# Slots of an expert in another order: neighbouring places nine slots apart, from the other end in the second expert of a pair

## The chip, the cores and the metric

One Trainium2 chip, one of its cores. The metric is device time in microseconds (us) of one execution; the median of three runs of the kernel before is 708.25 us (707.63 to 709.4).

## The reference

One decoder block on 512 tokens of width 1024: an mLSTM branch and a differential-attention branch run beside each other and are merged, then comes a mixture of experts routed in two levels. The change touches only the last part, whose core is:

```python
g_idx = top_k(softmax(hf @ w_rg + b_rg), 1)          # one of 4 groups
j_idx = top_k(softmax(e_logits of that group), 2)    # two of its 8 experts
combine = sum(one_hot(e_idx, 32) * weights)
for e in range(32):
    act = silu(hf @ w_gate[e]) * (hf @ w_up[e])      # 1024 -> 256, twice
    y = y + combine[:, e:e + 1] * (act @ w_down[e])  # 256 -> 1024
```

Every token goes to two of the 32 experts, so there are 1024 pairs of token and expert. All weights are float32: 3 MB an expert, 100 MB in all.

## The kernel before

The kernel runs as one program on one core. First come the projections, the two branches and the output projection, as float32 products split into a high and a low part; they end near 440 us. Then routing is worked out (to about 462 us), and then the experts run in 16 pairs. Pair i holds the experts `eA[i]` and `eB[i] = eA[i] + 8`, which lie in different groups, so that no token is in both.

For each expert there are 64 slots (`CAP`, `LIM`). A slot stands for a row of the pair's 128-row output tile `y`: the first expert has partitions 0 to 63, the second 64 to 127. `pos` holds, for each token and expert, the token's place among the tokens of that expert, 1, 2, 3 and so on (0 where it does not go there). `sio` holds for each slot the place that it takes: before, 1 to 64 in order. `places_of(i)` compares `pos` with `sio` on VectorE and makes the one-hot matrix `oh` with which TensorE gathers the columns of the tokens (`gather_mm`). An expert with n tokens thus fills its first n slots; the others hold zeros.

`one_hots` makes, once, the one-hot matrices `orb` from the places `rk` of each token's two choices, and `slots` multiplies them with a small table `ev6` to get, for each slot of each pair, the token's row number (`ids`) and its weight (`wsl`). An empty slot gets the row number 1024.

For a pair (`experts`): 32 matmuls for gate and up into `gu`, SiLU on ScalarE, the product on VectorE, two transposes, then 8 matmuls with the down weights into two banks `o`, which VectorE scales into `y`. Between SiLU and the down product TensorE does the gather for pair i + 2. Then GpSimd issues an indirect DMA that adds the 128 rows of `y`, 4 KB each, to the rows `ids[:, i]` of the output in DRAM; a row number beyond 511 is skipped (`bounds_check`, `oob_is_err=False`). There are 16 such scatters.

The weights are loaded by SyncE (SP), 1 MB a load, six for a pair, in the order of use. Twenty tiles take them in turn; a load is issued when the tile's last reader is done, some 20 loads ahead of use at the beginning and 8 at the end (`ahead`). SP issues in order: a load that waits holds all behind it.

Around the change: `W2` hands out the seven small buffers of the pool `work` in turn. That pool is released before the experts, and the pool `moe` (two of the weight tiles, `y1`, the gathered columns) lies over it. `dc` is a pool for the dense stages; it is released before the output projection, and the tiles `y0` (x rows of the first 128 tokens, later one of the three `y`) and `wx0` lie over it. `brt` holds the 36 router biases and is read by one matmul in `mod2`.

Of the kernel before, what the change touches and what calls it, by code (L numbers as in the profile page):

```python
# [10 lines left out]
F32 = mybir.dt.float32  # L11
F32R = mybir.dt.float32r
BF = mybir.dt.bfloat16
# [3 lines left out]
ALU = mybir.AluOpType  # L17
# [11 lines left out]
LIM = 64  # L29
# [28 lines left out]
def block_kernel(ctx, tc, x, c, positions, w_ada, b_ada, norm1_w, w_in, b_igate, b_fgate, conv_w, conv_b,  # L58
# [3 lines left out]
    PE, V, S, G, SP = nc.tensor, nc.vector, nc.scalar, nc.gpsimd, nc.sync  # L62
# [5 lines left out]
    const = ctx.enter_context(tc.tile_pool(name="const", bufs=1))  # L68
# [3 lines left out]
    dc = tc.alloc_tile_pool(name="dense", bufs=1, side="right")  # L72
# [5 lines left out]
    def W2(name, shape, dt=F32):  # L78
        return wk.tile(shape, dt, name=name, tag="w2", bufs=7)
# [4 lines left out]
    def acc(name="acc"):  # L84
        return ps.tile([128, 512], F32, name=name, tag="acc", bufs=4)
# [82 lines left out]
    for i, w in enumerate((lam_q1, lam_k1, lam_q2, lam_k2)):  # L168
# [10 lines left out]
                    pattern=[[-1, 128]], channel_multiplier=1)  # L179
# [7 lines left out]
                    pattern=[[1, 128]], channel_multiplier=-1)  # L187
# [4 lines left out]
                    pattern=[[-1, 128]], channel_multiplier=1)  # L192
# [44 lines left out]

    io8 = const.tile([128, 8], F32, name="io8")
    G.iota(io8, pattern=[[1, 8]], base=-8, channel_multiplier=0, allow_small_or_imprecise_dtypes=True)
    sio = const.tile([128, 64], BF, name="sio")  # L240
    G.iota(sio, pattern=[[1, 64]], base=1, channel_multiplier=0, allow_small_or_imprecise_dtypes=True)
    if LIM < 64:
        G.memset(sio[:, LIM:], -1e6)
    pio = const.tile([128, 1], F32, name="pio")
    G.iota(pio, pattern=[[0, 1]], base=0, channel_multiplier=1, allow_small_or_imprecise_dtypes=True)
    tio = const.tile([128, 4], F32, name="tio")
# [4 lines left out]
                    pattern=[[1, 128]], channel_multiplier=-1)  # L251
# [27 lines left out]
    st = {}  # L279
# [562 lines left out]
    wr = const.tile([128, 8, 36], F32, name="wr")  # L842
    SP.dma_start(wr[:, :, 0:4], w_rg[0].rearrange("(j p) f -> p j f", p=128))
    SP.dma_start(wr[:, :, 4:36], w_re[0].rearrange("(j p) f -> p j f", p=128))
    brt = const.tile([1, 36], F32, name="brt")
    SP.dma_start(brt[:, 0:4], b_rg)
    SP.dma_start(brt[:, 4:36], b_re)
    gbc = []
# [495 lines left out]
    def dense():  # L1344
# [5 lines left out]
    bc = lambda ap, n: ap[:, :, None].to_broadcast([128, 4, n])  # L1350
# [3 lines left out]
    oh = {0: W2("oh", [128, 4, 128], F16),  # L1354
          1: st["y0"][:, 512:768].bitcast(F16).rearrange("p (t f) -> p t f", t=4)}
# [3 lines left out]
    def places_of(i, ts=slice(0, 4)):  # L1359
        n = ts.stop - ts.start  # L1360
        for h, e in enumerate((eA[i], eB[i])):
            V.tensor_tensor(oh[i if st.get("first") else 2][:, ts, h * 64:h * 64 + 64], sio[:, None, :].to_broadcast([128, n, 64]),  # L1362
                            pos[:, ts, e:e + 1].to_broadcast([128, n, 64]), op=ALU.is_equal)

    def columns_of(i):
# [51 lines left out]
    def first_places():  # L1417
        ranks(0)
        places_of(0, lo2)
        places_of(1, lo2)  # L1420
# [12 lines left out]
    ranks(2)  # L1433
    idle(W1[2], wm)
    places_of(0, hi2)
    weights()
    places_of(1, hi2)
# [10 lines left out]
    ys = [st["y0"], mo.tile([128, 1024], F32, name="y1"), gbc[0][:, 0]]  # L1448
# [14 lines left out]
    nmore = rt("nmore", [128, 1], I32)  # L1463


    orb = [ys[0][:, c * 128:c * 128 + 128].bitcast(BF).rearrange("p (t f) -> p t f", t=4) for c in range(2)]
    ev6 = [ys[1][:, c * 384:c * 384 + 384].bitcast(BF).rearrange("p (t n f) -> p t n f", t=4, n=6) for c in range(2)]
    wrf = wr.rearrange("p k f -> p (k f)")
    rk = wrf[:, 128:136].rearrange("p (a t) -> p a t", a=2)
# [28 lines left out]

    def one_hots():
        for c_ in range(2):  # L1500
            V.tensor_tensor(orb[c_], sio[:, None, :].to_broadcast([128, 4, 64]), bc(rk[:, c_], 64), op=ALU.is_equal)

    def slots():

        idp = st["idp"] = acc("idp")[:, 0:96].rearrange("p (n i) -> p n i", n=6)
        k = 0
        for t in range(4):
            for c_ in range(2):
                for h in range(2):
                    r_ = ev6[c_][:, t].rearrange("p n (a h j) -> p n a h j", a=2, h=2)[:, :, :, h]  # L1510
                    PE.matmul(idp[h * 64:(h + 1) * 64], orb[c_][:, t], r_, start=(k == 0), stop=(k == 7),
                              skip_group_check=True)
                k += 1

# [8 lines left out]
    def experts(first=False):  # L1523
# [15 lines left out]
        if first:  # L1539
            one_hots()  # L1540
            rounds()
        for i in range(16):
# [23 lines left out]
            if first and i == 0:  # L1566
                slots()
                slot_ids()
# [19 lines left out]
    with tc.For_i(0, more, 1):  # L1588
        V.tensor_scalar(rk, rk, -float(LIM), None, op0=ALU.add)
        V.tensor_scalar(pos, pos, -float(LIM), None, op0=ALU.add)  # L1590
        table()
        one_hots()
        slots()
        slot_ids()
        experts()
# [22 lines left out]
```

## Time and profile before

| what | value |
|---|---|
| median of three runs | 708.25 us |
| the profiled execution: time, and span of its instructions | 710.0 us, 708.2 us |
| mean granted TensorE clock | 0.988 of full speed |
| TensorE matmul busy | 676.4 us, 96% of the span |
| VectorE, ScalarE, GpSimd busy | 378.3, 234.4, 201.9 us |
| moved by DMA | 171.50 MB, mean 242 GB/s |
| of this by GpSimd's queue (scatters and a few small ones) | 5.28 MB, 3.7% of 16 engines over the span |

"PE" is TensorE's matmul, "PEld" its weight load, DVE VectorE, ACT ScalarE, POOL GpSimd, SPq the queue of SyncE. The DMA share is the mean busy share of the core's 16 DMA engines; packets that overlap can bring it above 1. Matmuls are pipelined, so their durations overlap. In a row of the timeline, the brackets hold the idle time of the engine before the instruction and what ended it.

### The profile page before, as it was taken

What the parts mean: (1) busy time and instruction counts of PE and PEld (TensorE: products, weight loads), DVE (VectorE), ACT (ScalarE), POOL (GpSimd) and SP (SyncE); (2) the same over time, 40 slices, a digit from 0 to 9 for tenths busy, and PEclk for the clock granted to TensorE, in tenths of its full rate; (3) what the DMA queues carried; (4) which work ended last, traced back from release to release, by engine and by line L of the source; (5) the groups of instructions that cost most, each with busy time, mean ns of one, the idle gap of its engine ahead of it and who ended that gap; (6) DMA issues with size and microseconds to landing.
All of it is one profiled execution on the core that took longest, in us unless ns stands there. A gap on an engine that the chain in (4) does not pass through costs nothing. (4 is left out here: it accounts for less than half of the span.)

```text
span 708.2 us, 11482 instructions
## 1 busy us (share of the span) xinstructions
PE 676.4 (96%) x4478; PEld 497.6 (70%) x4478; DVE 378.3 (53%) x767; ACT 234.4 (33%) x513; POOL 201.9 (29%) x208
## 2 busy tenths in 40 slices
PE   7999999999998999999999999899999999999972
PEld 4678877878777777778877888676667666766640
DVE  3557669766684467763696855853222332233211
ACT  5446772352442445543322234341111111111100
POOL 4213263436561213233244521431111121111100
PEclk9999999999999999999999999899999999999998
DMA  9974079225025011056646992898999999999981
GB/s 313 363 231 176 0 279 405 75 70 184 35 71 179 1 60 61 1 187 219 232 150 220 421 398 90 323 410 326 379 364 385 410 403 375 392 371 399 408 299 22
DMA packets 47402, 171.50 MB, mean 242 GB/s; under 512 B 8025, under 2 KB 16354, under 8 KB 33006
## 3 DMA queue, kind: packets, MB, share of 16 engines
q1 hardware_dynamic: 44526, 165.41, 60.4%
q0 software_dynamic: 2752, 5.28, 3.7%
q8 instruction: 37, 0.61, 0.3%
q14 instruction: 23, 0.19, 0.1%
q10 hardware_dynamic: 64, 0.02, 0.0%
HBM read 164.37 MB, written 10.51 MB: 247 GB/s over the span
## 5 line engine op out<-in xcount | busy, mean ns | idle before, releaser
L435 POOL TENSOR_TENSOR hl<-wp,hl 128x512 fp32r<-128x512 f32 x60 | 84.8, 1414 | 174.1 <-ACT hl L434 165.5
L434 ACT ACTIVATE hl<-wp 128x512 fp32r<-128x512 f32 x120 | 74.5, 628 | 102.0 <-PE acc L492 42.9
L1549 PE MATMUL gu<-we,he 128*64 128x256 f32 x784 | 93.2, 379 | 0.5 <-DMA we<-in_w_gate 0.5
L491 PE MATMUL acc<-hTh,hl 128*128 128x512 f32 x220 | 90.4, 411 | 0.1
L493 PE MATMUL acc<-hTh,hl 128*128 128x512 f32 x220 | 87.6, 398 | 0.0
L492 PE MATMUL acc<-hTl,hl 128*128 128x512 f32 x220 | 87.3, 397 | 0.0
L1549 PEld LDWEIGHTS gu<-we,he 128*64 128x64 f32 x784 | 59.4, 137 | 34.0 <-issue 6.8
L435 DVE TENSOR_TENSOR hl<-wp,hl 128x512 fp32r<-128x512 f32 x60 | 53.5, 892 | 50.0 <-ACT hl L434 49.8
L1375 PEld LDWEIGHTS <-xn 128*128 128x128 f16 x1024 | 61.5, 115 | 6.9 <-issue 5.4
L1553 ACT ACTIVATE sg<-gu 128x256 f32<-128x256 f32 x16 | 6.2, 385 | 173.4 <-PE gu L1549 173.4
L1375 PE MATMUL gp<-oh,xn 128*128 128x128 f16 x960 | 60.9, 223 | 0.4 <-DVE oh L1362 0.4
L1581 POOL DMA_INDIRECT out<-y,wr x11 | 19.4, 1763 | 140.2 <-DVE y L1576 112.8
L1554 DVE TENSOR_TENSOR sg<-sg,gu 128x256 f32<-128x256 f32 x16 | 6.8, 423 | 95.2 <-ACT sg L1553 95.2
L495 PE MATMUL acc<-hl,hTh 128*128 128x512 f32 x128 | 52.6, 411 | 0.0
L491 PEld LDWEIGHTS acc<-hTh,hl 128*128 128x128 f32 x220 | 41.8, 190 | 14.9 <-issue 4.7
L497 PE MATMUL acc<-hl,hTl 128*128 128x512 f32 x128 | 50.2, 392 | 0.0
L496 PE MATMUL acc<-hl,hTh 128*128 128x512 f32 x128 | 50.1, 391 | 0.0
L1574 PE MATMUL o<-we,sg 128*64 128x512 f32 x192 | 48.2, 598 | 1.1 <-issue 1.1
L493 PEld LDWEIGHTS acc<-hTh,hl 128*128 128x128 f32 x220 | 41.7, 190 | 10.0
L492 PEld LDWEIGHTS acc<-hTl,hl 128*128 128x128 f32 x220 | 41.8, 190 | 8.6
L860 DVE SCALAR_TENSOR_TENSOR wada<-wada,ccols 128x1024 f32<-128x1024 f32 x28 | 41.5, 1506 | 1.7 <-DMA wada<-in_w_ada 1.6
L1393 DVE TENSOR_SCALAR he<-gp,AB 128x128 f32<-128x128 f32 x64 | 21.9, 403 | 23.4 <-PE gp L1375 18.4
(362 smaller groups left out, 1174.9 us busy)
## 6 DMA issues: line engine op xcount, KB each, us to landing
we<-in_w_gate SPq DMA_DIRECT2D x25, 1024.0 KB
we<-in_w_up SPq DMA_DIRECT2D x24, 1024.0 KB
we<-in_w_down SPq DMA_DIRECT2D x24, 1024.0 KB
wp<-in_w_in SPq DMA_DIRECT2D x20, 1024.0 KB
wada<-in_w_ada SPq DMA_DIRECT2D x16, 1024.0 KB
ada<-in_w_ada SPq DMA_DIRECT2D x16, 512.0 KB
wx<-in_w_gate SPq DMA_DIRECT2D x6, 1024.0 KB
wp<-in_w_out SPq DMA_DIRECT2D x4, 1024.0 KB
```

The lines of the kernel that those rows point to most:

```text
L434: S.activation(hi, src, AF.Copy)
L435: (G if LP(n) else V).tensor_sub(lo, src, hi.bitcast(F32))
L491: PE.matmul(g.banks[b], wh[:, sl], ah, start=st, stop=False)
L492: PE.matmul(g.banks[b], wh[:, sl], al, start=False, stop=False)
L493: PE.matmul(g.banks[b], wl[:, sl], ah, start=False, stop=en)
L495: PE.matmul(g.banks[b], ah[:, sl], wh, start=st, stop=False)
L496: PE.matmul(g.banks[b], ah[:, sl], wl, start=False, stop=False)
L497: PE.matmul(g.banks[b], al[:, sl], wh, start=False, stop=en)
L860: V.scalar_tensor_tensor(t0[:, sl], cur[:, sl], ccol[:, j:j + 1], t0[:, sl], op0=ALU.mult, op1=ALU.add)
L1375: PE.matmul(ps_[c_][:, jj * 128:(jj + 1) * 128], parts_of(t, part)[:, c_, :, jj], o[:, t], start=first and part is xnh and jj == 0 and t = ...
L1549: PE.matmul(gu[r, k * 256:(k + 1) * 256], h[:, j, r], wt[key, e][:, j], start=(j == 0), stop=(j == 7), skip_group_check=True)
L1574: PE.matmul(o[r], aT[:, j, r], wt["d", e][:, j, n * 512:(n + 1) * 512], start=(j == 0), stop=(j == 1), skip_group_check=True)
```

## The change

The table `sio` gets two rows of 64, one for each expert of a pair. For the first expert, slot 8a + b takes place 1 + 8a - 7b (plus 64 where that is below 1), so that place p + 1 lies nine slots behind place p: 1 is in slot 0, 2 in slot 9, 3 in slot 18. For the second expert it is 8 - 8a + 7b, the same order counted from slot 63 down. Every place has one slot as before; which rows of `y` are filled is another set. The table is made on GpSimd near the beginning, with a scratch tile `siw` from the ring of `W2`. `orb` has two matrices for each choice instead of one. `brt` moves from the pool `const` to the pool `dc`.

```diff
-    sio = const.tile([128, 64], BF, name="sio")
-    G.iota(sio, pattern=[[1, 64]], base=1, channel_multiplier=0, allow_small_or_imprecise_dtypes=True)
+    sio2 = const.tile([128, 2, 64], BF, name="sio")
+    siw = W2("siw", [128, 2, 64], BF)
+    for h in range(2):
+        G.iota(sio2[:, h], pattern=[[(8, -8)[h], 8], [(-7, 7)[h], 8]], base=(1, 8)[h], channel_multiplier=0,
+               allow_small_or_imprecise_dtypes=True)
+    G.tensor_scalar(siw, sio2, 0.5, 64.0, op0=ALU.is_lt, op1=ALU.mult)
+    G.tensor_add(sio2, sio2, siw)
     if LIM < 64:
-        G.memset(sio[:, LIM:], -1e6)
+        G.tensor_scalar(siw, sio2, LIM + 0.5, -1e6, op0=ALU.is_gt, op1=ALU.mult)
+        G.tensor_add(sio2, sio2, siw)
...
-    brt = const.tile([1, 36], F32, name="brt")
+    brt = dc.tile([1, 36], F32, name="brt")
...
-            V.tensor_tensor(oh[i if st.get("first") else 2][:, ts, h * 64:h * 64 + 64], sio[:, None, :].to_broadcast([128, n, 64]),
+            V.tensor_tensor(oh[i if st.get("first") else 2][:, ts, h * 64:h * 64 + 64], sio2[:, h, None].to_broadcast([128, n, 64]),
...
-    orb = [ys[0][:, c * 128:c * 128 + 128].bitcast(BF).rearrange("p (t f) -> p t f", t=4) for c in range(2)]
+    orb = [[ys[0][:, k:k + 128].bitcast(BF).rearrange("p (t f) -> p t f", t=4) for k in (c * 128, 768 + c * 128)]
+           for c in range(2)]
...
-            V.tensor_tensor(orb[c_], sio[:, None, :].to_broadcast([128, 4, 64]), bc(rk[:, c_], 64), op=ALU.is_equal)
+            for h in range(2):
+                V.tensor_tensor(orb[c_][h], sio2[:, h, None].to_broadcast([128, 4, 64]), bc(rk[:, c_], 64), op=ALU.is_equal)
...
-                    PE.matmul(idp[h * 64:(h + 1) * 64], orb[c_][:, t], r_, start=(k == 0), stop=(k == 7),
+                    PE.matmul(idp[h * 64:(h + 1) * 64], orb[c_][h][:, t], r_, start=(k == 0), stop=(k == 7),
```

`LIM` is 64, so the lines under `if LIM < 64` are not run.

## Rows read from the trace of the kernel before

**Rows 1.** Windows, one pair; us, busy per engine, PEclk, DMA share, GB/s
```profile
484.30:498.60 14.30, 14.30 (x148) 9.39 (x146) 4.38 (x10) 1.90 (x5) 1.57 (x1) 1.00 1.01 374
```

**Rows 2.** Waits from 470 us: who for what, us, times, longest
```profile
PE gu L1549 <- DMA wx<-in_w_up: 1.3, 1, 1.3
...
PE gu L1549 <- DMA we<-in_w_gate: 0.5, 1, 0.5
```

**Rows 3.** Windows where weight loads run dry, before any scatter
```profile
423.00:424.00 1.00, 1.00 (x6) 0.83 (x5) 1.00 (x3) 0.00 (x0) 0.00 (x0) 1.00 0.71 295
424.00:426.00 2.00, 2.00 (x11) 1.63 (x10) 0.21 (x1) 0.63 (x1) 0.89 (x1) 1.00 0.08 33
```

**Rows 4.** Windows across the end of the last weight loads
```profile
684.00:686.00 2.00, 1.02 (x10) 0.42 (x6) 0.00 (x0) 0.00 (x0) 0.00 (x0) 1.00 0.92 254
686.00:688.00 2.00, 1.69 (x16) 1.18 (x18) 0.00 (x0) 0.00 (x0) 0.00 (x0) 1.00 0.32 94
688.00:690.00 2.00, 1.98 (x18) 1.01 (x14) 0.00 (x0) 0.00 (x0) 0.00 (x0) 1.00 0.24 80
690.00:693.00 3.00, 1.53 (x6) 0.73 (x8) 0.85 (x2) 0.38 (x1) 0.00 (x0) 1.00 0.08 33
```

**Rows 5.** All scatters, issue to landing; then windows over the last one
```profile
DMA to landing us min/median/max: 5.6/10.5/11.1
...
699.00:702.00 3.00, 0.00 (x0) 0.00 (x0) 0.00 (x0) 0.00 (x0) 0.05 (x1) 0.91 0.62 89
...
702.00:702.50 0.50, 0.00 (x0) 0.00 (x0) 0.00 (x0) 0.00 (x0) 0.00 (x0) 0.50 0.13 25
```

**Rows 6.** Timeline of the last two pairs: start, us, engine, line
```profile
667.67 0.38 PE L1549 MATMUL gu<-ws,he 128*64 128x256 f32 x1
...
674.82 0.38 ACT L1553 ACTIVATE sg<-gu 128x256 f32<-128x256 f32 x1 [11.03 <-PE gu L1549]
...
676.78 3.65 PE L1574 MATMUL o<-we,sg 128*64 128x512 f32 x16 [0.56 <-issue]
680.24 0.59 PE L1549 MATMUL gu<-we,he 128*64 128x256 f32 x2
681.34 3.45 PE L1549 MATMUL gu<-we,he 128*64 128x256 f32 x29 [0.51 <-DMA we<-in_w_gate]
...
686.31 0.43 PE L1549 MATMUL gu<-wx,he 128*64 128x256 f32 x1 [1.30 <-DMA wx<-in_w_up]
...
690.02 0.38 ACT L1553 ACTIVATE sg<-gu 128x256 f32<-128x256 f32 x1 [14.81 <-PE gu L1549]
...
691.98 4.45 PE L1574 MATMUL o<-we,sg 128*64 128x512 f32 x16 [0.56 <-issue]
```

**Rows 7.** Timeline of GpSimd: start, us, engine, line
```profile
11.27 0.18 POOL L241 IOTA sio<- 128x64 bf16 x1
...
17.94 1.29 POOL L435 TENSOR_TENSOR hl<-wp,hl 128x512 fp32r<-128x512 f32 x1 [5.78 <-ACT hl L434]
...
456.40 0.41 POOL L1426 TENSOR_TENSOR wr<-rtmp 128x128 bf16<-128x128 f32 x1 [3.05 <-DVE rtmp L1311]
```

**Rows 8.** Timeline of VectorE around the slot one-hots
```profile
466.38 1.05 DVE L1501 TENSOR_TENSOR y<-sio,wr 128x256 bf16<-128x256 bf16 x2
...
470.41 0.42 DVE L1554 TENSOR_TENSOR sg<-sg,gu 128x256 f32<-128x256 f32 x1 [2.69 <-ACT sg L1553]
```

**Rows 9.** The load of the first x rows; the matmul on `brt`
```profile
385.85 0.35 SPq L1058 DMA_DIRECT2D y<-in_x  x1
...
L908 PE MATMUL rbp<-brt,ones x2: 274/284/294, 390.4 to 390.6; 1*128 1x36 f32 x2
```

**Rows 10.** Timeline of SP's queue around the loads into pool `moe`
```profile
445.69 1.21 SPq L1104 DMA_DIRECT2D we<-in_w_gate  x2
...
447.99 1.17 SPq L1104 DMA_DIRECT2D ws<-in_w_down  x2
453.38 0.80 SPq L1104 DMA_DIRECT2D wx<-in_w_gate  x2
```

## The prediction, made before the change was run

> **What bounds the kernel now.** I read the windows of the expert stage first. The reader is to see that TensorE is busy for the whole stretch of a pair and that, in the same stretch, the 16 DMA engines are full too (share 1.01) [rows 1]. Two resources are saturated, so the next view decides: what TensorE waits for. From 470 us on its matmuls wait for DMA only twice, both times on weights of the last pair of experts [rows 2]. Weights are loaded far ahead at first, the stock is used up over sixteen pairs, and it runs out in the last one.
>
> Then the DMA share across that end. When the same weight loads run dry earlier, with no scatter in sight, the share falls from 0.71 to 0.08 within some two microseconds [rows 3]: the engines finish together. At the end of the expert stage it does not: 0.92, then 0.32, 0.24 and 0.08 over nine microseconds [rows 4]. 0.32 of 16 is five engines, still moving weights after eleven have finished. What lies between the two ends is sixteen scatters, so I look at the last one, which runs alone: after 702 us its share is 0.13, two engines [rows 5], although 62 tokens over 16 engines would be four apiece.
>
> The tokens per expert I counted by running the reference's router on its inputs: 16 to 44, 1024 in all; the last pair has 39 and 23. A slot without a token has an index out of bounds and moves next to nothing. Today the filled slots are 0 to 38 and 64 to 86. If an engine serves partitions in fours (0 to 31 of a half over eight engines, 32 to 63 over the same eight again, the other half over the other eight), this scatter gives engines of 8, 7, then four each, 3, 0 and 0 rows: two go on alone, as rows 5 show. Summed over all scatters the sixteen engines get 90, 74, 65, 64, 57, 49, 37, 32 and 99, 86, 80, 64, 64, 63, 55, 45. Five lie above 65, which is the five of rows 4. So the late weights are late because a load has landed only when its slowest engine is done, and five engines carry more scatter rows than the rest.
>
> The Trainium skill (DMA: Bandwidth & Descriptors, The descriptor swizzle) gives engine = 8*(p>>6) + ((p>>2)&7), the deal just inferred; by it the trace agrees, and no row here names an engine.
>
> **The change part by part.** The sum is made against the profiled execution: 710.0 us, of which 708.2 are span. The median shown is 708.25, 1.75 below it, and I carry that offset over.
>
> Even rows. With the new order the same deal gives 64, 56, 63, 54, 61, 55, 61, 54 and 65, 74, 64, 73, 64, 76, 65, 75. The work of the engines is the same, so first the landing with a perfect deal: 2 x 0.92 + 2 x 0.32 + 2 x 0.24 + 3 x 0.08 = 3.2 us of all sixteen engines are left from 684 on [rows 4], hence 687.2. Today the last load is there at about 692.75 (the down matmuls start at 691.98 and take 4.45 instead of 3.65 us [rows 6]), 5.55 us late for 35 rows above the mean of 64, that is 0.16 us a row. The new largest sum is 76, 12 above the mean: 1.9 us, so 689.1.
>
> When are the weights wanted? Pair 14 shows the pace without a stall: first gate matmul 667.67, SiLU 674.82, 7.15 us [rows 6]. Pair 15 takes 680.24 to 690.02, 9.78 us: 2.63 us of standing. Without it the down matmuls would start at 691.98 - 2.63 = 689.35, just behind 689.1. The up weights now allow the matmul at 686.31; 5.55 earlier and 1.9 later is 682.7, wanted at 680.24 + 7.15 / 2 = 683.8. The gate weights, now at 681.34, come at 677.7, wanted at 680.24. All three hide, the last by only a quarter of a microsecond. Gain: 2.63 plus the 0.80 in the down matmuls, 3.43 us. What is late next is TensorE itself, gapless [rows 1], so nothing more is to be had from even engines.
>
> Last scatter. It lands 5.6 us after its issue, alone; the others take 10.5 in the median [rows 5]. Its fullest engine drops from 8 to 5 rows. A row is worth 0.16 us by the tail above, or 0.62 x 3 x 16 / 62 = 0.48 us when all engines begin together [rows 5]: 0.5 to 1.4 us for three. I take 0.7, near the lower end, because the long engines work with little beside them at the end.
>
> New slot numbers. On POOL one iota (0.18) becomes two, and a tensor_scalar and a tensor_add on 128x128 are added; the nearest row is the 0.41 us of a 128x128 product: about +1.0 us [rows 7]. Up to 2 us if iotas start slower; it only adds, so no gain. Behind it stand the other constants and the first split, and POOL idles 5.78 us before that: nothing. Without that cover it would be 1.0 us on the first projection.
>
> One-hots. Two more VectorE operations of the kind that takes 1.05 us for two. VectorE idles 2.69 us before the first gate product [rows 8]: nothing. The token one-hots and the slot matmuls keep their number and shapes.
>
> The bias row in another pool. The tile of the x rows lies over the released pool, and its load starts at 385.85, right after the last reader there. The bias row is read by the matmul at 390.4 to 390.6 [rows 9]: SP stands up to 5 us longer, and behind it the x loads and the first expert weights. They end 3 to 5 us later; the engines are empty from 425 on (0.08) [rows 3], so I cost it at nothing. Without that cover it would be the 5 us.
>
> The scratch tile takes a turn in the ring of seven small buffers, so the tiles laid over that ring later may lie over others. What hangs on this is the pair of gate loads at 453.38, at which SP stands [rows 10]. Lower bound nothing. Upper: SP waits for the last one-hot read, at the end of the first gather near 462. Six loads of 1.05 MB are issued in three pairs from 445.69 on [rows 10]; at 374 GB/s [rows 1] that is 2.8 us each, work to about 462.5. So the engines would stand for little more than the start of a load; I bound it by one load's time, 2.8 us, less the quarter microsecond of slack: +2.5 us. I take 0, because the engines have work for all of the likely hold.
>
> Sum: 710.0 - 2.63 - 0.80 - 0.7 = 705.9, and as a median 705.9 - 1.75 = **704.1 us**.
>
> **The rivals.** Another deal: single partitions in turn. Then today's sums are 82 to 51 and the new ones 75 to 52: of 18 rows above the mean 11 remain, so the lateness falls only from 5.55 to 3.4 us. Gate hides; up comes 0.4 us, down 0.8 us late, and the last scatter keeps 5 rows: 710.0 - 2.2 = 707.8, median 706.0. Against it: that scatter would not leave two engines alone.
>
> The gate loads held up, as above, by half to all of that bound: 705.4 to 706.6. For it: the lists of what lies over what are not in the profile. Against it: it needs the latest reader of all under those two tiles.
>
> The change does not do what it says, since the tail is not the rows' but that of a queue delayed otherwise (scatter 14 is itself issued into the tail at 681.5): waits stay, only the last scatter gains: 707.5 to 708.3. For it: the price of 0.16 us a row is far from the 0.48 of a scatter alone. Against it: five engines and two engines, both as counted.
>
> Slower: an engine that is slow at scatter rows gets more of them. Engine 15 goes from 45 to 75 rows, engine 7 from 32 to 54. If 15 is today's last one, with fewer rows than the mean, its 30 more rows cost 30 x 0.16 = 4.8 to 30 x 0.48 = 14.4 us at the end of the loads, and the down matmuls wait for them: 714.8 to 724.4, median from 713.0. It decides from the point where its last load lands after 692.75, today's landing. Against it: by count the five late engines are explained without a slow one. The Trainium skill (DMA: Bandwidth & Descriptors, Latency and other measured facts) says that engines 7 and 15 are usually slower than the others, with the scatter's descriptor rings as its best guess; by that rule this rival would be the outcome. The drain of the loads alone [rows 3] shows no such engine; while scatters run, no row tells them apart.
>
> **How the numbers follow.** About 0.3%, 2.1 us, is what a measurement of this kernel can tell from no change. Forecast (703.0 to 705.3): 0.58. Gate loads held up (705.4 to 706.6): 0.10. Single partitions (706.0, at the border): 0.08. Waits stay (707.5 to 708.3): 0.14. Slow engine (713 and more): 0.07. More than forecast, below 703: 0.03. Faster by over 0.3% (below 706.1) takes the first, half of the second and third, and the last: 0.70; slower is 0.07; the rest, 0.23, within. The range of 702.8 to 707.6 leaves out the slow engine, most of the waits that stay and the far end below.
>
> **What would show it.** In the profile after: no matmul of the last pair waits on DMA; the time from its first gate matmul to its SiLU is near 7.15 us, the down matmuls near 3.65; the DMA share falls from above 0.9 to under 0.1 within about three microseconds; the last scatter lands in 4.7 to 5.1 us; POOL's first split still begins on ScalarE's word near 17.9; the gate loads of the fourth pair are issued near 453. A tail of one or two engines that reaches beyond 692 would make me wrong on the slow side; a tail as long as today's would say that the rows are not its cause.

## The result, and the profile after

The changed kernel takes 704.53 us (median of 4 runs, 703.04 to 705.96) beside 708.68 us (707.63 to 709.4) for the kernel before: a ratio of 0.9945, interval 0.993 to 0.9961. The prediction was 704.1 us, faster. The profiled execution after took 705.96 us with a span of 704.2 us; before, 710.0 and 708.2. Line numbers have moved by eight to ten (gate and up matmuls L1559, SiLU L1563, down matmuls L1584, scatter L1591).

The waits of TensorE from 470 us on, kernel after (who for what, us in total, times, longest). The two DMA rows of [rows 2] are not there; what is left is not DMA:

```profile
PE pa L1570 <- DVE sg L1564: 1.9, 2, 1.0
PE o L1584 <- issue: 1.1, 2, 0.6
```

The timeline of the last two pairs, kernel after (start, us, engine, line), to be laid beside [rows 6]:

```profile
667.37 0.38 PE L1559 MATMUL gu<-ws,he 128*64 128x256 f32 x1
...
674.52 0.38 ACT L1563 ACTIVATE sg<-gu 128x256 f32<-128x256 f32 x1 [11.04 <-PE gu L1559]
676.49 3.65 PE L1584 MATMUL o<-we,sg 128*64 128x512 f32 x16 [0.56 <-issue]
679.94 3.65 PE L1559 MATMUL gu<-we,he 128*64 128x256 f32 x32
...
687.09 0.39 ACT L1563 ACTIVATE sg<-gu 128x256 f32<-128x256 f32 x1 [12.18 <-PE gu L1559]
689.05 3.65 PE L1584 MATMUL o<-we,sg 128*64 128x512 f32 x16 [0.56 <-issue]
...
693.78 1.54 POOL L1591 DMA_INDIRECT out<-y,wr  x1 [11.03 <-DVEq L1598]
```

Both pairs now run at the same pace: 667.37 to 674.52 and 679.94 to 687.09, 7.15 us each, where the last one took 9.78. The last down matmuls take 3.65 instead of 4.45 us. The 4.0 us between the two spans can be read off step by step, by how much earlier each point is than in [rows 6]: the down matmuls of pair 14 by 0.29 us (676.49 for 676.78; the stage simply began that much earlier), the last SiLU by 2.93 (2.63 of standing are gone), the last scatter by 3.71 (697.49 in the kernel before; some 0.8 from the down matmuls), the end of the span by 4.0 (0.3 from the scatter itself).

The windows across the end of the weight loads, kernel after (us, busy per engine, PEclk, DMA share, GB/s):

```profile
682.00:684.00 2.00, 2.00 (x22) 1.61 (x20) 0.00 (x0) 0.00 (x0) 0.75 (x1) 1.00 1.03 420
684.00:686.00 2.00, 2.00 (x22) 1.57 (x20) 0.00 (x0) 0.00 (x0) 0.00 (x0) 1.00 0.88 277
686.00:688.00 2.00, 1.07 (x11) 0.53 (x7) 0.42 (x1) 0.39 (x1) 0.00 (x0) 1.00 0.34 82
688.00:690.00 2.00, 1.44 (x8) 0.76 (x10) 0.42 (x1) 0.00 (x0) 0.00 (x0) 1.00 0.05 12
```

1.03, 0.88, 0.34, 0.05, where [rows 4] fell over nine microseconds. The engines finish much closer together, though not as close as in [rows 3]: in half-microsecond windows of the same trace the share is 0.96 from 685.0 and 0.09 from 688.0.

The last scatter, kernel after: all scatters from issue to landing, then the windows over the last one, for [rows 5]:

```profile
DMA to landing us min/median/max: 5.3/10.0/11.6
```

```profile
695.30:698.00 2.70, 0.00 (x0) 0.00 (x0) 0.00 (x0) 0.00 (x0) 0.03 (x1) 0.90 0.77 97
698.00:698.50 0.50, 0.00 (x0) 0.00 (x0) 0.00 (x0) 0.00 (x0) 0.00 (x0) 0.50 0.23 49
698.50:699.00 0.50, 0.00 (x0) 0.00 (x0) 0.00 (x0) 0.00 (x0) 0.00 (x0) 0.50 0.01 0
```

The two engines that went on alone (0.13) are gone: the share is high to the end and then drops. But it lands only 0.3 us sooner (5.3 for 5.6); 4.7 to 5.1 was forecast.

Last, what was costed at nothing: GpSimd's start, VectorE's one-hots and SP's queue, in the timeline of the kernel after, for [rows 7 to 10]:

```profile
11.42 0.87 POOL L245 IOTA sio<- 128x64 bf16 x2
12.38 0.68 POOL L247 TENSOR_SCALAR siw<-sio 128x128 bf16<-128x128 bf16 x1
13.13 0.43 POOL L248 TENSOR_TENSOR sio<-sio,siw 128x128 bf16<-128x128 bf16 x1
...
18.27 1.29 POOL L443 TENSOR_TENSOR hl<-wp,hl 128x512 fp32r<-128x512 f32 x1 [4.29 <-ACT hl L442]
...
389.93 0.35 SPq L1066 DMA_DIRECT2D y<-in_x  x1
452.46 0.86 SPq L1112 DMA_DIRECT2D wx<-in_w_gate  x2
...
465.42 1.51 DVE L1511 TENSOR_TENSOR y<-sio,wr 128x256 bf16<-128x256 bf16 x4
...
470.05 0.42 DVE L1564 TENSOR_TENSOR sg<-sg,gu 128x256 f32<-128x256 f32 x1 [2.82 <-ACT sg L1563]
```

GpSimd's three steps take 1.98 us in place of 0.18, and it still idles 4.29 us before the first split, waiting for ScalarE (the split starts 0.33 us later than before because ScalarE does). VectorE still idles 2.82 us. The x load is issued 4.1 us later (389.93 for 385.85); the gate loads of the fourth pair at 452.46, not later than before.

### The profile page after: what moved, and what is told of

It reads as the page before. It is cut to its first block, busy times and chain, and to the rows that moved or that the text cites. A ratio compares the mean times of both kernels' runs of the same rounds, so it can differ in the third digit from the quotient of the medians.

```text
span 704.2 us, 11486 instructions
## 1 busy us (share of the span) xinstructions
PE 674.9 (96%) x4478; PEld 498.1 (71%) x4478; DVE 378.1 (54%) x769; ACT 234.3 (33%) x513; POOL 202.1 (29%) x211
## 5 line engine op out<-in xcount | busy, mean ns | idle before, releaser
L1559 PE MATMUL gu<-we,he 128*64 128x256 f32 x784 | 92.6, 379 | 0.0
L1559 PEld LDWEIGHTS gu<-we,he 128*64 128x64 f32 x784 | 59.7, 137 | 32.5 <-issue 6.8
L1563 ACT ACTIVATE sg<-gu 128x256 f32<-128x256 f32 x16 | 6.2, 385 | 170.7 <-PE gu L1559 170.7
L1591 POOL DMA_INDIRECT out<-y,wr x11 | 19.3, 1756 | 140.2 <-DVE y L1586 116.2
L1584 PE MATMUL o<-we,sg 128*64 128x512 f32 x192 | 47.4, 598 | 1.1 <-issue 1.1
```

Of the source, the lines that this page charges most:

```text
L1559: PE.matmul(gu[r, k * 256:(k + 1) * 256], h[:, j, r], wt[key, e][:, j], start=(j == 0), stop=(j == 7), skip_group_check=True)
L1584: PE.matmul(o[r], aT[:, j, r], wt["d", e][:, j, n * 512:(n + 1) * 512], start=(j == 0), stop=(j == 1), skip_group_check=True)
```

## The experiments

All are edits of the changed kernel; "..." marks what is cut. The first four touch only the lines that number the slots, so that everything else of the change stays in. They ran with the kernel before on one chip (708.25 us, 706.39 to 709.83, 20 runs).

**e1_old_order: all of the change but the order.**

```diff
-        G.iota(sio2[:, h], pattern=[[(8, -8)[h], 8], [(-7, 7)[h], 8]], base=(1, 8)[h], channel_multiplier=0,
+        G.iota(sio2[:, h], pattern=[[8, 8], [1, 8]], base=1, channel_multiplier=0,
                allow_small_or_imprecise_dtypes=True)
```

> The kernel after, with the slots of both experts in the old order again (places 1 to 64 in slots 0 to 63); the two tables, the scratch tile, the doubled one-hots and the bias row's pool stay as in the kernel after. Theory (the order alone evens the scatter rows over the DMA engines, the other edits cost nothing): the time of the kernel before, 708 to 709.5 us; the fullest engine has 99 rows again, the tail of the weight loads reaches 692 to 693, the last pair takes 9.4 to 9.9 us from its first gate matmul to SiLU. Rival (the other edits brought part of the gain, for example the later x loads or other tiles under the weight tiles): 704 to 707 us with a long tail, or a short tail with the old order.

Measured: 707.93 us (10 runs), ratio 0.9992, interval 0.9981 to 1.0004. The waits of TensorE from 470 us on, and the windows across the end of the loads, with the old order; between them, from the timeline, when TensorE goes on with the gate and the up weights of the last pair:

```profile
PE gu L1559 <- DMA wx<-in_w_up: 1.3, 1, 1.3
...
PE gu L1559 <- DMA we<-in_w_gate: 0.5, 1, 0.5
```

```profile
680.18 3.45 PE L1559 MATMUL gu<-we,he 128*64 128x256 f32 x29 [0.51 <-DMA we<-in_w_gate]
...
685.13 0.43 PE L1559 MATMUL gu<-wx,he 128*64 128x256 f32 x1 [1.28 <-DMA wx<-in_w_up]
```

```profile
684.00:686.00 2.00, 0.87 (x8) 0.63 (x10) 0.00 (x0) 0.00 (x0) 0.00 (x0) 1.00 0.47 131
686.00:688.00 2.00, 2.00 (x22) 1.30 (x19) 0.00 (x0) 0.00 (x0) 0.00 (x0) 1.00 0.28 82
688.00:690.00 2.00, 1.07 (x8) 0.54 (x4) 0.42 (x1) 0.38 (x1) 0.00 (x0) 1.00 0.14 57
690.00:692.00 2.00, 1.44 (x6) 0.43 (x7) 0.42 (x1) 0.00 (x0) 0.00 (x0) 1.00 0.06 20
```

[rows 2] come back to the tenth, and the tail with them. The two iotas, the wrap, the second set of one-hots, the bias row's pool and the ring's extra turn together cost nothing and bring nothing that these runs can tell (0.3 us less than the kernel before, interval 1.3 less to 0.3 more); the order is the gain.

**e2_crowded: an order worse than the old one.** The slots are filled engine by engine: the first eight places go to slots 0 to 3 and 32 to 35, which by the deal one engine serves, the next eight to the next engine's. By the same count four engines get 127 or 128 rows, where the fullest of the old order gets 99.

```diff
-        G.iota(sio2[:, h], pattern=[[(8, -8)[h], 8], [(-7, 7)[h], 8]], base=(1, 8)[h], channel_multiplier=0,
-               allow_small_or_imprecise_dtypes=True)
+        for a in range(2):
+            G.iota(sio2[:, h, a * 32:a * 32 + 32], pattern=[[8, 8], [1, 4]], base=1 + 4 * a, channel_multiplier=0,
+                   allow_small_or_imprecise_dtypes=True)
```

> The kernel after, with places 1 to 8 of each expert in the slots 0 to 3 and 32 to 35, places 9 to 16 in 4 to 7 and 36 to 39, and so on. If engines serve partitions in fours as counted, the engines of each half get 128, 128, 106, 69, 36, 1, 0, 0 and 128, 128, 127, 100, 57, 16, 0, 0 rows: the worst order there is. Theory: 64 rows above the mean instead of 35, so the last load is late by 64 x 0.16 = 10 us instead of 5.5 at the price of the tail (713 us), by 64 x 0.48 = 31 us at the price of a scatter alone (734 us). Rival, single partitions in turn: the fullest engine has 93 rows, about as many as the 82 of the old order, 709 to 711 us. Rival, the tail is not made by rows: 704 to 709 us.

Measured: 719.5 us (718.3 to 720.39), ratio 1.0154, interval 1.0129 to 1.0179. The waits of TensorE from 470 us on, windows over its tail, and two matmuls of pair 14 from the timeline:

```profile
PE gu L1560 <- DMA we<-in_w_up: 2.3, 2, 1.3
PE gu L1560 <- DMA we<-in_w_gate: 2.0, 2, 1.3
...
PE gu L1560 <- DMA wx<-in_w_gate: 1.8, 1, 1.8
PE gu L1560 <- DMA wx<-in_w_up: 1.5, 2, 1.3
```

```profile
694.00:696.00 2.00, 0.92 (x9) 0.63 (x11) 0.00 (x0) 0.00 (x0) 0.00 (x0) 1.00 0.44 121
...
700.00:702.00 2.00, 1.24 (x4) 0.19 (x2) 0.42 (x1) 0.00 (x0) 0.00 (x0) 1.00 0.13 53
```

```profile
672.41 0.43 PE L1560 MATMUL gu<-wx,he 128*64 128x256 f32 x1 [1.76 <-DMA wx<-in_w_gate]
...
674.26 0.63 PE L1560 MATMUL gu<-wx,he 128*64 128x256 f32 x1
```

The tail ends on 0.13, two engines where the count would leave four, and earlier pairs wait too. An order can thus also make the kernel 11.6 us slower than the old one, which the rivals "single partitions" and "not the rows'" cannot give: by the first, this order would be hardly worse, by the second, the same. The price is 11.6 us for 29 more rows on the fullest engine, 0.40 us a row; the tail's 0.16 was too low for it, the lone scatter's 0.48 too high. Nor is it a price of rows alone: after the stand of 1.76 us the granted clock fell to 0.50 (its lower level, 1.2 GHz) from about 672.8 to 676, and matmuls that start 0.21 us apart at full clock started 0.43 apart. That is 1.7 us of slower work in this profile, some of it perhaps hidden by the next wait, for the up weights.

**e3_reversed: the old order from the other end.** Within each 32 slots the groups of four are filled from the far end, so that the engines which got 90 and 99 rows get few and those which got few get 90 and 99.

```diff
-        G.iota(sio2[:, h], pattern=[[(8, -8)[h], 8], [(-7, 7)[h], 8]], base=(1, 8)[h], channel_multiplier=0,
-               allow_small_or_imprecise_dtypes=True)
+        for a in range(2):
+            G.iota(sio2[:, h, a * 32:a * 32 + 32], pattern=[[-8, 4], [-1, 8]], base=32 + 32 * a, channel_multiplier=0,
+                   allow_small_or_imprecise_dtypes=True)
```

> The kernel after, with place p in slot 32 - p (p up to 32) or 96 - p (above): the old crowding mirrored, so that the engines get 32, 37, 49, 57, 64, 65, 74, 90 and 45, 55, 63, 64, 64, 80, 86, 99 rows. Engine 7, which had 32 rows, has 90, and engine 15, which had 45, has 99. Theory (all engines alike, only the fullest counts): as the old order, 708 to 709.5 us. Rival (engines 7 and 15 are slower than the rest at scatter rows): 711 us or more, with a tail beyond 695. Rival (engines 0 and 8 are the slow ones, and the old order put the rows there): below 707 us.

Measured: 710.49 us (708.75 to 712.74, 10 runs), ratio 1.0035, interval 1.0019 to 1.0052: 2.6 us above e1, with the same counts. The timeline of the last pair, then windows over it; its profiled execution is near the upper end of its runs (712.09):

```profile
675.48 3.91 PE L1585 MATMUL o<-we,sg 128*64 128x512 f32 x16 [0.56 <-issue]
...
681.59 3.45 PE L1560 MATMUL gu<-we,he 128*64 128x256 f32 x29 [1.79 <-DMA we<-in_w_gate]
...
687.46 0.69 PE L1560 MATMUL gu<-wx,he 128*64 128x256 f32 x1 [2.20 <-DMA wx<-in_w_up]
```

```profile
686.00:688.00 2.00, 0.54 (x4) 0.35 (x6) 0.00 (x0) 0.00 (x0) 0.00 (x0) 0.84 0.34 107
688.00:690.00 2.00, 2.00 (x12) 1.11 (x10) 0.00 (x0) 0.00 (x0) 0.00 (x0) 0.50 0.16 61
```

Counted from the down matmuls of pair 14 (675.48 here, 675.62 in e1), the gate weights are there after 6.1 us (4.6 in e1: 680.18) and the up weights after 12.0 (9.5: 685.13). So in these two profiles the loads end 1.5 to 2.5 us later when the same crowd of rows goes to the other end. That is none of the three expected: the ends are not alike, the median lies just below the 711 us of the slow engines and the tail ends before 693, and the difference is far from what a slow engine was priced at (4.8 us at the least). The rest of this profile's loss is the clock. After the second stand its granted clock falls to 0.50, the 1.2 GHz level, and the first matmul takes 0.69 us where 0.38 to 0.43 is the rule; in e1 the stands were 0.5 and 1.3 us and the clock stayed at 1.00. Of the other nine runs of e3 one has a mean clock as low as this one's 0.984 (712.74 us); the rest have 0.986 to 0.989, which the kernel before has too, so the 2.6 us between the medians need not hold this loss.

The Trainium skill (DMA: Bandwidth & Descriptors, Latency and other measured facts) says that engines 7 and 15 are usually slower than the others; by its deal (The descriptor swizzle, stated there for a plain transfer to 128 partitions) these two carry the 90 and 99 rows of this order. The later loads agree in sign. No row of a trace names an engine, so whether it is these engines or something else of the reversed order stays open.

**e4_same_end: the new order, both experts from the same end.**

```diff
-        G.iota(sio2[:, h], pattern=[[(8, -8)[h], 8], [(-7, 7)[h], 8]], base=(1, 8)[h], channel_multiplier=0,
+        G.iota(sio2[:, h], pattern=[[8, 8], [-7, 8]], base=1, channel_multiplier=0,
                allow_small_or_imprecise_dtypes=True)
```

> The kernel after, with the second expert of a pair counted from the same end as the first (nine slots apart in both). By fours the halves are served by different engines, the fullest engine has 76 rows as in the kernel after. Theory: the same time, 703.5 to 705.5 us, tail ending 687 to 689. Rival, single partitions in turn: the fullest has 82 rows instead of 75, a little slower, 705 to 707 us.

Measured: 704.64 us (703.89 to 706.16, 5 runs), ratio 0.9956, interval 0.9939 to 0.9974: the same as the changed kernel. The windows across the end of the loads:

```profile
682.00:684.00 2.00, 2.00 (x22) 1.61 (x20) 0.00 (x0) 0.00 (x0) 0.00 (x0) 1.00 0.75 211
684.00:686.00 2.00, 1.07 (x8) 0.44 (x4) 0.42 (x1) 0.38 (x1) 0.00 (x0) 1.00 0.25 68
686.00:688.00 2.00, 1.44 (x8) 0.74 (x9) 0.42 (x1) 0.00 (x0) 0.00 (x0) 1.00 0.04 12
```

There is no wait on DMA and no long tail. Which end the second expert starts from does not matter: the two experts' slots lie on different engines by the deal, so mirroring one can't even out the other. By single partitions the fullest engine would have 82 rows again, as in the old order; nothing of that shows.

**e5_old_one_scatter and e6_new_one_scatter: the last scatter by itself.** They leave out the scatters of the first 15 pairs, e5 on e1 and e6 on the changed kernel, with the kernel before at 707.03 us (706.72 to 709.73, 7 runs) on their chip.

```diff
-            G.indirect_dma_start(out=out2, out_offset=bass.IndirectOffsetOnAxis(ap=ids[:, i:i + 1], axis=0),
+            if i == 15:
+                G.indirect_dma_start(out=out2, out_offset=bass.IndirectOffsetOnAxis(ap=ids[:, i:i + 1], axis=0),
...
```

> The old order (as e1_old_order), with the scatters of the first 15 pairs left out, so their part of the sum is missing from the output; only the last pair's scatter is issued, with 8 rows on its fullest engine. Theory (the tail is made of scatter rows, and behind it TensorE is the bound): the weight loads end together, within 2 us, no matmul waits for DMA, the last pair takes 7.15 us to SiLU; 708.0 - 3.4 = 704.6 us, 703.5 to 705.5. Rival (the tail belongs to the weight loads themselves): a tail of several microseconds and 707 to 708 us although 15 scatters are gone.

> The kernel after, with the scatters of the first 15 pairs left out in the same way. Theory (after the change the scatters cost nothing beside the last one, TensorE is the bound): the time of the kernel after, 703.5 to 705.5 us, although 15 of 16 scatters and their 962 rows are gone. Rival (scatters still cost time through the loads that they delay): 698 to 702 us. Beside e5_old_one_scatter it also prices the last scatter: 5 rows on the fullest engine here, 8 there; 0.5 to 1.4 us by the prediction, about 0.3 us by the landings of the kernel after (5.3 against 5.6 us).

Measured: 702.89 us (701.26 to 703.35, ratio 0.9924, interval 0.9894 to 0.9954) and 701.52 us (700.75 to 703.3, ratio 0.9909, interval 0.988 to 0.9937). First the end of the loads in windows, in e5 and then in e6:

```profile
680.00:682.00 2.00, 2.00 (x22) 1.61 (x20) 0.00 (x0) 0.00 (x0) 0.00 (x0) 1.00 0.76 315
682.00:684.00 2.00, 2.00 (x22) 1.61 (x20) 0.00 (x0) 0.00 (x0) 0.00 (x0) 1.00 0.09 37
```

```profile
682.00:684.00 2.00, 2.00 (x22) 1.59 (x20) 0.00 (x0) 0.00 (x0) 0.00 (x0) 1.00 0.46 193
684.00:686.00 2.00, 2.00 (x22) 1.58 (x19) 0.00 (x0) 0.00 (x0) 0.00 (x0) 1.00 0.14 57
```

With the old order and no scatter beside the loads, 0.76 falls to 0.09 at once and the last pair doesn't wait: without the scatters the nine microseconds of [rows 4] are gone. That the scatters delay the loads is shown by this; that it is their uneven rows, and not just their amount, is shown by e1 beside the changed kernel, since e5 takes away both. Nor is every slow end theirs: in e6, also without scatters, one to four engines go on from 683 to 686 (0.14 over the last two microseconds), for a reason that no row shows. So an end of three to four microseconds, as in the kernel after, is by itself no sign of uneven rows. The last scatter's landing, e5 and then e6:

```profile
DMA to landing us min/median/max: 6.1/6.1/6.1
```

```profile
DMA to landing us min/median/max: 5.4/5.4/5.4
```

With 8 rows on the fullest engine 6.1 us, with 5 rows 5.4: 0.7 us. The medians, 1.4 us apart on few runs, neither confirm nor exclude that size.

The runs lie 1.7 us (e5) and 3.1 us (e6) below the 704.6 that was expected, and e6 falls into the 698 to 702 of its rival, scatters that still cost time through the loads. But the rival's mechanism isn't seen, for the difference isn't in the expert stage. From the first SiLU of the stage to the issue of the last scatter, the kernel after takes 224.16 us (469.62 to 693.78), e5 224.18 (468.56 to 692.74) and e6 224.17 (469.18 to 693.35). Behind the issue of the last scatter 1.6 us (e5) and 2.3 us (e6) are missing beside the kernel after, as the section on the hardware tells; the rest of e6's miss, 0.8 us, is within what the start of the expert stage moves.

## Why the prediction was right, point by point

One number sums up the runs: the time between the SiLUs of the last two pairs (674.82 and 690.02 in [rows 6]).

| kernel | rows on the fullest engine, by count | SiLU to SiLU, us | time, us |
|---|---|---|---|
| before | 99 | 15.20 | 708.68 |
| e1, old order | 99 | 15.19 | 707.93 |
| e3, old order reversed | 99 | 19.26 | 710.49 |
| e2, crowded | 128 | 16.28 (earlier pairs wait too) | 719.5 |
| after | 76 | 12.57 | 704.53 |
| e4, same end | 76 | 12.57 | 704.64 |
| e5, e6, last scatter only | 8, 5 | 12.56 | 702.89, 701.52 |

**What bounds it.** Right. 12.57 us is TensorE without a wait, and no even order gets below it: e4 and the kernel after agree to the hundredth, and taking nearly all scatters away (e5, e6) doesn't shorten the stage either.

**The even rows.** Right: 3.43 us were forecast for the standing and the stretched down matmuls, and 2.63 and 0.8 are what the timeline shows. The step that the forecast rested on, the deal of four partitions to an engine, was inferred from two windows; e2, which crowds exactly the engines of that deal, bears it out with 11.6 us and a handful of engines left at its end (0.32, 0.18, 0.13).

**The landing.** The last load was forecast for 689.1, wanted at 689.35. The engines move data until about 689.0 (0.07 in the half microsecond before, 0.00 in the one after), and the down matmuls start at 689.05 without a wait. So the landing came out as forecast, and by these rows the margin is no wider than the quarter of a microsecond; how much of the last data is weights and how much is scatter 14, issued at 681.21, no row shows. The row's price of 0.16 us was of the right order at the end of the loads, but it is not a constant. It came from the end of one stage; in e2, where the stock of weights runs out pairs earlier and each late load also delays the next and the clock falls once, a row on the fullest engine costs 0.40.

**The last scatter.** Here the size was off. 0.7 us were forecast; after its issue the kernel after is 0.3 us shorter than before, and beside e1 0.4 (5.3 for 5.7). The landings of the other runs agree: 5.6 to 5.9 with 8 rows on the fullest engine (before, e1, e2, e3), 5.3 and 5.4 with 5 (after, e4). Only without the other scatters, e5 beside e6, is the difference the 0.7. The term assumed that fewer rows on the fullest engine shorten the scatter in proportion. In [rows 5] the engines were busy for (0.62 x 3 + 0.13 x 0.5) x 16 = 30.8 us together; now it is (0.77 x 2.7 + 0.23 x 0.5) x 16 = 35.1 us for the same 62 rows, 0.57 instead of 0.50 us a row. That would mean that rows take longer when more engines work side by side, so that even rows take away the long engines and give part of it back. The sign holds in the other traces, the size doesn't: summed in half microseconds from the issue to the end of the span, it is 29.1 us in e2, 33.3 before, 33.7 in e1, 34.6 in e4 and 37.0 after. Why a row takes longer is not shown.

**The hidden costs.** Right by e1: all of them together 0.9992. GpSimd's addition was taken as 1.0 us with a bound of 2; it was 1.8, the two iotas 0.87 instead of the 0.18 that one took in [rows 7]. It hides as named, under the wait for ScalarE, of which 4.29 us are left. SP's stand before the x load is the 4.1 us foreseen, and the weight loads behind it run dry later, hidden as said (a share of 1.03 from 424 to 426, where [rows 3] have 0.08, and no wait of TensorE for DMA from 470 us on). The gate loads weren't held up (452.46).

**The rivals.** Single partitions fall with e2 and e4, "the tail is not the rows'" with e2 and e5. The gate loads held up falls with the profile after. The slow engine falls at its price: engine 15 by the count went from 45 to 75 rows without a wait, and e3, with all 99 there, costs 2.6 us. Its sign may not be wrong, though: with the crowd of rows at that end the loads came 1.5 to 2.5 us later in the two profiles, for a cause that is open.

**The offset.** The sum was made against an execution 1.75 us above the median, and the forecast of 704.1 lies 0.4 below the result. The start of the expert stage moves by 2 to 3 us between the profiled executions of these kernels (its first SiLU at 469.99 before, 467.16 in e4), so this is within what the runs scatter. That the total came so close is in part luck: of the forecast 4.13 us the profiles show 3.4 in the loads and 0.3 in the last scatter, and an earlier start of the stage, which the change did not make, filled in most of the missing 0.4.

## What to carry to other kernels

When a rows-by-partition transfer has partly filled tiles, count how many filled rows each DMA engine gets over all transfers: a load has landed only when its fullest engine has, so an uneven count shows as a DMA share that steps down over many microseconds (nine here; in e6 the loads alone took three) instead of dropping. Permuting the slots costs a few operations on a constant, and it pays only if the late loads are waited for; here that was one pair in sixteen, 3.4 of 708 us. Once the engine that bounds the stage has no wait left, a still better order brings nothing.

## What the runs showed of the hardware

**The end of the program depends on the scatters behind it.** The windows from the last scatter to the end of the span, kernel after:

```profile
700.00:702.00 2.00, 0.00 (x0) 0.00 (x0) 0.00 (x0) 0.00 (x0) 0.00 (x0) 0.50 0.02 4
702.00:704.20 2.20, 0.00 (x0) 0.00 (x0) 0.00 (x0) 0.00 (x0) 0.00 (x0) 0.50 0.00 0
```

And of e6, the same order with one scatter:

```profile
698.00:698.50 0.50, 0.00 (x0) 0.00 (x0) 0.00 (x0) 0.00 (x0) 0.00 (x0) 0.50 0.05 16
...
700.00:701.50 1.50, 0.00 (x0) 0.00 (x0) 0.00 (x0) 0.00 (x0) 0.00 (x0) 0.50 0.02 5
```

After: data until some time before 699, end at 704.2, and next to nothing moves in the more than 5 us between. e6: data until some time before 698.5, end at 701.5, little more than 3. From the landing of the last scatter to the end of the span it is 5.1 or 5.2 us in all six kernels with 16 scatters, whatever their order, and 2.8 in e5 and e6. From the issue of the last scatter it is 10.42 us to the end in the kernel after, 8.86 in e5 and 8.15 in e6. So some 2.4 us at the end come with the 15 scatters before the last one and not with the last one itself. Whether they grow with the number, and what the chip does in them, no row shows; a kernel with half the scatters would be the next thing to try.

**A stand of TensorE can cost twice.** In e3 a wait of 2.2 us was followed by a granted clock of 0.50; from the release of the up weights to the SiLU it took 5.3 us (687.46 to 692.78), where e1 took 3.7 (685.13 to 688.84). In e2 the same followed a stand of 1.76 us, with matmuls of 0.63 us. Not every stand does it: the 1.79 us before the gate weights of e3 left the clock at 1.00. The kernel before lost nothing in this way: its stands were shorter (0.51 and 1.30 us) and its clock stayed at 1.00 [rows 4].
